# One core, a hybrid attention and mLSTM layer: three engines keep the source's order through the attention stretch

## The chip, the core and the metric

The kernel runs on one core of a Trainium2 chip. A core has a TensorE for matrix products (PE in the profile, its weight loads PEld), a VectorE (DVE), a ScalarE (ACT), a GpSimd (POOL) and a SyncE (SP), which issues the DMAs. Each of them works through its own list of instructions in the order in which they stand in it, and waits at an instruction until the semaphores that it names are there. The metric is the time of one execution on the device in microseconds (us); the figure for a kernel is the median of its runs.

## What is computed

A sequence of 2048 rows of 1024 numbers goes through one layer, in float32:

```python
h = rmsnorm(x, norm_g)
u = h @ w_in                                   # 1024 -> 7168, cut into q_a k_a v_a z_a x_m o_m z_m
# A: 8 heads of 128; three dilated causal windows, merged by their softmax denominators
att = sum(softmax(lses) * outs) * silu(z_a)
# B: 4 mLSTM heads of 256, chunk by chunk, with a state C handed on
num = inter * (q_t @ C) + p @ v_t
hm = sigmoid(o_m) * num / max(|den|, exp(-m_t))
hm = (hm - mean(hm)) * rsqrt(var(hm) + 1e-6) * hn_g
mls = hm * silu(z_m)
y = x + concat(att, mls) @ w_out
out = rmsnorm(y, final_g)
```

## The kernel before

The work has four stages. First the input projection with its normalisation, by seven products per block (the loop over `stream`); its results go to DRAM (`q_d`, `k_d`, `v_d`, `za_d`, `qm_d`, `xc_d`, `o_d`, `zm_d` and others). It ends at about 1241 us of the trace.

Second, attention beside the mLSTM, to about 1720 us. `attention` is a generator that runs through 256 units, 32 for each of 8 heads (16 blocks `b` for the local pattern, R = 0, and 16 for the dilated ones, R = 1, in turn). A unit `i` passes three steps: `qk` makes the scores (three products into a `pq` bank, L748 to L750), VectorE adds the bias and takes the row minimum (L752), ScalarE takes the exponential (L754); two units later `flip` transposes the result on TensorE (L762, into a `pt` bank) and ScalarE (L767) or VectorE (L765) copies it to `p`; one unit later `pv` multiplies it with the values (L780, into a `pm` bank). Of `pq`, `pt`, `pm` and `pu` there are two PSUM banks each. Once in eight units `qk_split` cuts the next quarter of q and k into a high and a low part: ScalarE makes the high ones (L620, L625), VectorE the low ones (L621, L626), GpSimd reorders q (L623). Per head, `head_stats` and `head_merge` combine the two patterns (L793 to L844).

`mlstm` is a second generator, stepped inside the first one's loop (L1243 and the lines behind it): 16 chunks of 128 rows, each in two `unit`s of nine pieces. A unit takes an exponential on ScalarE (`E`, L957, of what GpSimd cut out of `nb`, L944), products of q and k (L962, into `pt`), a transpose (L970) scaled by ScalarE into `kw` (L974), the outputs (L982, L985, into `pu`), which VectorE gates into `hm` (L986 to L990), and the new state `C` (L997 on TensorE, L1000 on VectorE). `norm`, run as `tail` beside the next chunk, normalises a chunk: small VectorE operations on `sm`, four squares on ScalarE (L1020), an inverse square root by three Newton steps of [128, 4] (L85 to L94), four multiplications of [128, 256] (L1031), and two sets of transposes (L1036, L1037).

Third, to about 2040 us, `early`: the mLSTM half of the output projection, block by block (L1142 to L1144, three products per piece), stepped beside the last attention units. It loads weights and mLSTM results into the two buffers `wor`, splits them on ScalarE and VectorE (L98, L99) into `we` and `me`, and from unit 230 on `load_wo` brings the weights of the other half, through the same two buffers. Fourth, the attention half and the last normalisation.

The generators fix only the order of the source. In what order the instructions of one engine are then listed is chosen by a list scheduler that knows the dependencies and its own estimate of each duration. The source also has a function `keep_order(start, engines)`, which chains all instructions of an engine behind `start` in source order; here it is called for the projection's start alone, with no engine in its list (`KO = ()`), so nothing is chained.

Of the kernel before, what the change touches and what calls it, by code (L numbers as in the profile page):

```python
# [8 lines left out]
F32 = mybir.dt.float32  # L9
# [18 lines left out]
def kernel(  # L28
# [52 lines left out]
    def rsqrt(pool, v, n):  # L81
# [5 lines left out]
        for c in (3.0, 12.0, 768.0):  # L87
            if n == 1:
                nc.vector.tensor_scalar(t, y, y, v, op0=ALU.mult, op1=ALU.mult)
            else:  # L90
                nc.vector.tensor_tensor(t, y, y, ALU.mult)
                nc.vector.tensor_tensor(t, t, v, ALU.mult)
            nc.vector.scalar_tensor_tensor(y, t, c, y, op0=ALU.subtract, op1=ALU.mult)
        nc.vector.tensor_scalar(y, y, -1.0 / 8192.0, None, op0=ALU.mult)  # L94
# [608 lines left out]
    def head_tiles(at, d):  # L703
# [3 lines left out]
        for n, shape, bufs in (("vn", [128, 16, 128], 2), ("vc", [128, 16, 128], 2), ("zs", [128, T], 1)):  # L707
            d[n] = at.tile(shape, F32, name=n, bufs=bufs)
# [7 lines left out]
        nc.sync.dma_start(d["zs"], za_d[h])  # L716
# [71 lines left out]
    def head_stats(at, d):  # L788
        h = d["h"]
        ps = pt.tile([128, 512], F32, name="pt")  # L790
# [61 lines left out]
    def attention(at):  # L852
# [9 lines left out]
        for i in range(len(units) + 3):  # L862
            if i < len(units):
                h, u = units[i]
                if i == 0:
# [4 lines left out]
                    qk_split(D_[0], 0)  # L870
                S_[i] = qk(at, D_[h], u)
            if 0 <= i - 2 < len(units):
                h, u = units[i - 2]
                s, n = S_[i - 2]
                P_[i - 2] = flip(at, D_[h], u, s, n)
# [40 lines left out]
    def mlstm(mp):  # L916
# [90 lines left out]
        def norm(c):  # L1007
# [14 lines left out]
            yield  # L1022
# [3 lines left out]
            rs = rsqrt(mp, sm[:, 3, :], 4)  # L1026
            nc.vector.tensor_tensor(sm[:, 3, :], rs, sm[:, 1, :], ALU.mult)
            yield
            for h in range(MH):
                hm = hms[h // 2][:, h % 2]  # L1030
                nc.vector.tensor_scalar(hm, hm, sm[:, 0, h:h + 1], sm[:, 3, h:h + 1], op0=ALU.add, op1=ALU.mult)  # L1031
            yield
            for p in range(2):
# [4 lines left out]
                yield  # L1038
# [6 lines left out]
        for c in range(NB):  # L1045
            SM[c] = mp.tile([128, 4, MH], F32, name="sm", bufs=2)
            for p in range(2):
                nxt = (c, 1) if p == 0 else (c + 1, 0)
                for n, _ in enumerate(unit(c, p, nxt if nxt[0] < NB else None)):
                    yield  # L1050
                    if tail and n % 2:
                        if next(tail, "end") == "end":
                            tail = None
                        else:
                            yield
# [6 lines left out]
    def raw_tile():  # L1062
# [3 lines left out]
        return woB.tile([128, 512], F32, name="wor", bufs=2)  # L1066
# [12 lines left out]
    def load_wo(e):  # L1079
        pool, tag, bufs = ((at, "vn", 2), (at, "vc", 2), (ax[0], "kh", 1), (pre, "k", 1),  # L1080
                           (at, "oL", 2), (at, "oR", 2), (at, "vn", 2), (at, "vc", 2))[e]
        t = pool.tile([128, 2, D], F32R, name=tag, bufs=bufs)
        for n in range(2):
            c = slice(n * 512, (n + 1) * 512)
            raw = raw_tile()
            nc.sync.dma_start(raw, w_out[e * 128:(e + 1) * 128, c])
            split(t[:, 0, c], t[:, 1, c], raw)
# [4 lines left out]
    def early():  # L1092
# [16 lines left out]
        def m_split(n, b, i):  # L1109
            t = M[n, b, i] = woB.tile([128, 2, 4, 128], F32R, name="me", bufs=3)  # L1110
# [8 lines left out]
        w_get(0, 0)  # L1119
        m_get(0, 0, 0)  # L1120
        w_split(0, 0)
        m_split(0, 0, 0)
        yield 0
        for e in range(1, 8):
            w_get(0, e)
            if e == 4:
                m_get(0, 0, 1)
                w_split(0, e)
                m_split(0, 0, 1)
            else:  # L1130
                w_split(0, e)
            if e % 2:
                yield 0
# [58 lines left out]
    def out_fin(pss, b):  # L1192
        xr = at.tile([128, 2, D], F32, name="zs")[:, 0] if b % 2 == 0 else at.tile([128, D], F32, name="wr")
# [22 lines left out]
    def out_last(pss, b):  # L1216
        xr = at.tile([128, 2, D], F32, name="zs")[:, 0] if b % 2 == 0 else at.tile([128, D], F32, name="wr")
        nc.sync.dma_start(xr, y_d[b * 128:(b + 1) * 128, :])
        s2 = at.tile([128, 2], F32, name="s2", bufs=2)
        for n in range(2):  # L1220
# [6 lines left out]
            if n == 0:  # L1227
# [9 lines left out]
    total, done, start, end, lag = 16 * 25, 0, 18, 180, 3  # L1237
# [5 lines left out]
                            ident[:8, 4:8, None].to_broadcast([8, 4, 128]), ALU.add)  # L1243
    work = attention(at)
# [22 lines left out]
    for _ in work:  # L1267
# [7 lines left out]
        i += 1  # L1275
    loads += [load_wo(e) for e in range(4, 8)]
# [86 lines left out]
```

## Time and profile before

| | |
|---|---|
| median of 3 runs | 2219.49 us (2218.13 to 2221.97) |
| the profiled execution | 2220.11 us, of which 2217.2 us are the span from first to last instruction |
| PE busy | 2126.7 us (96% of the span) |
| DVE busy | 1488.1 us (67%) |
| ACT busy | 942.8 us (43%) |
| POOL busy | 251.8 us (11%) |
| mean granted TensorE clock | 0.988 of 2.4 GHz |

A PE that is called busy need not be at its peak, since the ends of its records are modelled and a record that waits inside its span counts as busy. So the number of records in a stretch says more than the busy time, where the mixture is alike. The granted clock has two levels, 1.2 and 2.4 GHz; a mean of 0.87 over a stretch means that the lower one held for about a quarter of it.

### The profile page before, as it was taken

To read this page: it belongs to the slowest core of one execution; us is meant where nothing else is said; L and a number is where in the kernel's file an instruction comes from. 1 tells how busy PE (TensorE), PEld (TensorE's weight loads), DVE (VectorE), ACT (ScalarE), POOL (GpSimd) and SP (SyncE) were. 2 spreads that over 40 slices of the span, in tenths; PEclk is the share of its full clock that TensorE was granted. 3 is DMA by queue.
4 is the path that set the end of the run, shared out by engine and by line. 5 is a ranking of instruction groups with operands and counts; after the bars stand their busy time and mean duration, and the time that the engine had idled before them with its cause. 6 is when DMAs were issued, how large, how long until landed. Compare 5 with 4: busy or idle time off the path is not lost.

```text
span 2217.2 us, 32676 instructions
## 1 busy us (share of the span) xinstructions
PE 2126.7 (96%) x11826; PEld 1788.0 (81%) x11826; DVE 1488.1 (67%) x3050; ACT 942.8 (43%) x1905; POOL 251.8 (11%) x221
## 2 busy tenths in 40 slices
PE   5999999999999999999999999999898999999998
PEld 4777888998878888787779888888887788777886
DVE  8887768556696558576666578868777644643654
ACT  6433333333383223334344555655555645532221
POOL 2200000000000000000000223343342221210000
PEclk9999999999999999999999999999999999999999
DMA  4256343432263333343324677776675664565442
GB/s 154 95 177 190 114 159 115 158 114 101 90 204 133 114 114 105 125 138 115 133 77 160 186 203 208 213 234 188 195 211 178 192 184 157 173 193 176 162 138 86
DMA packets 278896, 341.52 MB, mean 154 GB/s; under 512 B 22224, under 2 KB 194704, under 8 KB 276688
## 3 DMA queue, kind: packets, MB, share of 16 engines
q1 hardware_dynamic: 277872, 338.85, 48.2%
q8 instruction: 93, 1.52, 0.3%
q10 hardware_dynamic: 864, 0.59, 0.1%
q14 instruction: 67, 0.55, 0.1%
HBM read 222.13 MB, written 117.24 MB: 153 GB/s over the span
## 4 chain that ended last, share of the span: by engine, by line
PE 74%; DVE 9%; DMA 8%; issue 5%; ACT 3%; POOL 1%; SPq 0%; ACTq 0%; DVEq 0%; POOLq 0%
PE pb L349 31%; PE pa L349 12%; PE pm L780 3%; PE pu L997 2%; PE pt L762 2%; PE pu L985 2%; DMA wor<-mls_d 2%; DMA wor<-in_w_out 1%; DMA k<-k_d 1%; PE aux L500 1%; PE aux L510 1%; PE pq L748 1%; PE pq L750 1%; PE pq L749 1%; PE pu L982 1%
## 5 line engine op out<-in xcount | busy, mean ns | idle before, releaser
L98 ACT ACTIVATE whi<-ws 128x1024 fp32r<-128x1024 f32 x140 | 148.2, 1059 | 376.5 <-PE pb L349 209.4
L99 DVE TENSOR_TENSOR wlo<-ws,whi 128x1024 fp32r<-128x1024 f32 x140 | 171.8, 1227 | 81.3 <-ACT whi L98 80.4
L139 DVE TENSOR_TENSOR ws<-w,w 128x1024 f32<-128x1024 f32 x140 | 172.1, 1229 | 24.0 <-DMA w<-in_w_in 22.4
L754 ACT ACTIVATE s<-s,st 128x256 f32<-128x256 f32 (+3 forms) x256 | 134.9, 527 | 76.0 <-DVE st L752 68.8
L411 DVE TENSOR_TENSOR o<-pb,o 128x1024 f32<-128x1024 f32 x84 | 102.8, 1224 | 92.9 <-PE pb L349 91.9
L752 DVE CUSTOM_DVE_ANT_0 s<-pq,bl 128x256 f32<-128x256 f32 (+3 forms) x256 | 114.2, 448 | 43.3 <-PE pq L750 32.0
L612 POOL COPY bl<-bl 128x256 f32<-128x256 f32 x8 | 6.4, 796 | 1150.5 <-DMA q<-q_d 1111.3
L767 ACT ACTIVATE p<-pt 128x256 f32<-128x256 f32 (+1 forms) x192 | 81.3, 424 | 105.7 <-PE pt L762 104.6
L762 PE MATMUL pt<-sc,s 128*128 128x128 f32 x568 | 107.7, 279 | 7.1 <-ACT p L767 5.3
L98 ACT ACTIVATE whi<-w 128x1024 fp32r<-128x1024 f32 x56 | 59.2, 1057 | 125.2 <-PE pb L349 118.7
L1142 PE MATMUL pu<-we,me 128*128 128x512 f32 x256 | 106.6, 417 | 5.3 <-ACT me L98 4.4
L411 DVE TENSOR_TENSOR o<-pa,o 128x1024 f32<-128x1024 f32 x56 | 68.4, 1221 | 62.8 <-PE pa L349 62.8
L1143 PE MATMUL pu<-we,me 128*128 128x512 f32 x256 | 102.1, 399 | 2.9 <-DVE me L99 2.9
L1144 PE MATMUL pu<-we,me 128*128 128x512 f32 x256 | 101.2, 395 | 0.0
L780 PE MATMUL pm<-p,vc 128*128 128x128 f32 x640 | 96.3, 281 | 3.3 <-DVE p L765 1.7
L404 ACT ACTIVATE o<-pb 128x1024 f32<-128x1024 f32 x84 | 84.9, 1016 | 15.6 <-DVE o L411 9.8
L780 PEld LDWEIGHTS pm<-p,vc 128*128 128x128 f32 x640 | 84.0, 195 | 7.0 <-ACT p L767 3.5
L99 DVE TENSOR_TENSOR wlo<-w,whi 128x1024 fp32r<-128x1024 f32 x56 | 68.3, 1220 | 27.5 <-ACT whi L98 27.5
L762 PEld LDWEIGHTS pt<-sc,s 128*128 128x128 f32 x568 | 72.7, 143 | 17.3 <-ACT p L767 6.7
L99 DVE TENSOR_TENSOR me<-wor,me 128x512 fp32r<-128x512 f32 x64 | 48.4, 758 | 56.0 <-ACT me L98 55.9
L780 PE MATMUL pm<-p,vn 128*128 128x128 f32 x496 | 78.7, 279 | 5.1 <-ACT p L767 5.1
L997 PE MATMUL pu<-v,kw 128*128 128x257 f32 x240 | 71.6, 401 | 9.4 <-DVE C L1000 4.8
(592 smaller groups left out, 6565.9 us busy)
## 6 DMA issues: line engine op xcount, KB each, us to landing
w<-in_w_in SPq DMA_DIRECT2D x112, 512.0 KB
wor<-mls_d SPq DMA_DIRECT2D x64, 256.0 KB
q_d<-o SPq DMA_DIRECT2D x8, 1024.0 KB
k_d<-o SPq DMA_DIRECT2D x16, 512.0 KB
vm_d<-vm SPq DMA_DIRECT2D x32, 256.0 KB
xc_d<-xc SPq DMA_DIRECT2D x32, 256.0 KB
qm_d<-qm SPq DMA_DIRECT2D x32, 256.0 KB
v_d<-o SPq DMA_DIRECT2D x8, 1024.0 KB
```

What stands on the lines that cost most here:

```text
L98: nc.scalar.activation(hi, raw, AF.Copy)
L99: nc.vector.tensor_tensor(lo, raw, f(hi), ALU.subtract)
L139: eng.tensor_tensor(s, a, b, ALU.add if sign > 0 else ALU.subtract)
L349: nc.tensor.matmul(out, lhsT, rhs, start=start, stop=stop, skip_group_check=True)
L411: nc.vector.tensor_tensor(dst, ps, src, op)
L752: nc.vector.tensor_tensor_reduce(s[:, :n], ps[:, :n], bias, 1.0, 3e38, ALU.add, ALU.min, accum_out=st[:, col:col + 1])
L754: nc.scalar.activation(s[:, :n], s[:, :n], AF.Exp, bias=st[:, col:col + 1], scale=-1.0, accum_out=st[:, 16 + col:17 + col])
L762: nc.tensor.transpose(pp[:, i * 128:(i + 1) * 128], s[:, i * 128:(i + 1) * 128], ident)
L780: nc.tensor.matmul(od, v, p[:, j * 128:(j + 1) * 128], start=j == 0, stop=j == m - 1)
L997: nc.tensor.matmul(u[:, 0:257], kw[:, 2 * i + e, :], v[:, i], start=True, stop=True)
L1142: nc.tensor.matmul(acc, m[:, 0, j], w[:, 0], start=e == 0, stop=False)
L1143: nc.tensor.matmul(acc, m[:, 1, j], w[:, 0], start=False, stop=False)
```

## The change

`keep_order` is called once more, behind the loop over the attention units, for TensorE, VectorE and ScalarE and all instructions since the first attention unit. GpSimd's and SyncE's lists are still the scheduler's. With it the source is written in another order:

- `flip` of unit i-2 stands ahead of `qk` of unit i.
- `norm` has 13 pieces where it had 7 (one Newton step or two multiplications in a piece), and each piece rides behind a piece of the next chunk's units, with no place of its own: a chunk now takes 18 places and not 25 (`total`).
- the gate tile `zs` is loaded in `head_stats`, when it is near its use.
- `load_wo` issues both its loads, lets two places pass, and then splits; it has two buffers of its own, `wol`. `me` has two buffers and not three.
- `early` asks for its first ten tiles two ahead of the split.

```diff
+    def rsqrt_steps(pool, v, n):
...
+        for c in (3.0, 12.0, 768.0):
+            nc.vector.tensor_tensor(t, y, y, ALU.mult)
+            nc.vector.tensor_tensor(t, t, v, ALU.mult)
+            nc.vector.scalar_tensor_tensor(y, t, c, y, op0=ALU.subtract, op1=ALU.mult)
+            yield
...
@@ head_tiles, head_stats
-        nc.sync.dma_start(d["zs"], za_d[h])
...
+        d["zs"] = at.tile([128, T], F32, name="zs")
+        nc.sync.dma_start(d["zs"], za_d[h])
@@ attention
+            if 0 <= i - 2 < len(units):
+                hf, uf = units[i - 2]
+                s, n = S_[i - 2]
+                P_[i - 2] = flip(at, D_[hf], uf, s, n)
+            if i < len(units):
                 S_[i] = qk(at, D_[h], u)
-            if 0 <= i - 2 < len(units):
-                h, u = units[i - 2]
-                s, n = S_[i - 2]
-                P_[i - 2] = flip(at, D_[h], u, s, n)
@@ norm
+            yield
             nc.vector.reciprocal(sm[:, 1, :], sm[:, 1, :])
...
-            yield
+                if h % 2:
+                    yield
...
-            rs = rsqrt(mp, sm[:, 3, :], 4)
+            yield
+            rs = yield from rsqrt_steps(mp, sm[:, 3, :], 4)
...
             for h in range(MH):
+                if h == 2:
+                    yield
@@ mlstm, the loop over the units
-                    if tail and n % 2:
-                        if next(tail, "end") == "end":
-                            tail = None
-                        else:
-                            yield
+                    if tail and next(tail, "end") == "end":
+                        tail = None
@@ raw_tile, load_wo
-        return woB.tile([128, 512], F32, name="wor", bufs=2)
+        return woB.tile([128, 512], F32, name="wol", bufs=2)
...
+        raw = [raw_tile() for _ in range(2)]
+        for n in range(2):
+            nc.sync.dma_start(raw[n], w_out[e * 128:(e + 1) * 128, n * 512:(n + 1) * 512])
+        yield
+        yield
@@ early
-            t = M[n, b, i] = woB.tile([128, 2, 4, 128], F32R, name="me", bufs=3)
+            t = M[n, b, i] = woB.tile([128, 2, 4, 128], F32R, name="me", bufs=2)
...
+        tiles = [("w", 0, e) for e in range(4)] + [("m", 0, 0, 0)] + [("w", 0, e) for e in range(4, 8)] + [("m", 0, 0, 1)]
+        for i in range(len(tiles) + 2):
+            if i >= 2:
+                (w_split if tiles[i - 2][0] == "w" else m_split)(*tiles[i - 2][1:])
+            if i < len(tiles):
+                (w_get if tiles[i][0] == "w" else m_get)(*tiles[i][1:])
+            if i % 2:
                 yield 0
@@ the main loops
-    total, done, start, end, lag = 16 * 25, 0, 18, 180, 3
+    total, done, start, end, lag = 16 * 18 + 14, 0, 18, 180, 3
...
+    begin2 = len(nc.cur_bb.bb.instructions)
     work = attention(at)
...
+    keep_order(begin2, (mybir.EngineType.PE, mybir.EngineType.DVE, mybir.EngineType.Activation))
```

Both kernels have the same instructions; only their order and some buffers differ. Three places follow. The lines of the changed kernel stand 12 to 21 below those of the kernel before.

VectorE in the second chunk's normalisation (L94 ends the inverse square root, L1031 is the four multiplications), before:

```order
L94 TENSOR_SCALAR rs_y_10953<-rs_y_10953 128x4
L989 SCALAR_TENSOR_TENSOR sm<-pu,gcol 128x1
L1000 SCALAR_TENSOR_TENSOR C<-C,decb,pu 128x257
L1027 TENSOR_TENSOR sm<-rs_y_10953,sm 128x4
L990 TENSOR_TENSOR sm<-sm,pu 128x1
L752 ISA s,st<-pq,bl 128x128
L752 ISA st 128x1
L765 COPY p<-pt 128x128
L1031 TENSOR_SCALAR hm<-hm,sm 128x256 x4
L1000 SCALAR_TENSOR_TENSOR C<-C,decb,pu 128x257 x2
L752 ISA s,st<-pq,bl 128x256
```

and now, where L108 is the old L94, L1052 the old L1031, L765 the old L752:

```order
L108 TENSOR_SCALAR rs_y_10997<-rs_y_10997 128x4
L1046 TENSOR_TENSOR sm<-rs_y_10997,sm 128x4
L1016 SCALAR_TENSOR_TENSOR C<-C,decb,pu 128x257
L1052 TENSOR_SCALAR hm<-hm,sm 128x256 x2
L778 COPY p<-pt 128x256
L765 ISA s,st<-pq,bl 128x256
L765 ISA st 128x1
L1052 TENSOR_SCALAR hm<-hm,sm 128x256 x2
L979 TENSOR_TENSOR E<-E,pt 128x256
L1058 TENSOR_TENSOR z<-z,pt 128x512
```

The four multiplications stood in one row, ahead of two state updates and of the next unit's minimum; now a unit's minimum stands between two and two.

ScalarE at the second `unit` of the third chunk (L957 is its `E`, L974 the `kw` of the unit ahead of it), at about 1316 to 1321 us of the trace before:

```order
L974 ACTIVATE kw<-pt,gcol 128x256 x2
L754 ACTIVATE s,st<-s,st 128x256
L957 ACTIVATE E<-E,gcol 128x128 x2
L767 ACTIVATE p<-pt 128x256
L620 ACTIVATE qh<-q 128x512
L625 ACTIVATE kh<-k 128x4x128
L754 ACTIVATE s,st<-s,st 128x128
```

and now (L973 the same `E`, L990 the `kw` of its own unit):

```order
L796 ACTIVATE oR<-pm 128x4x128
L973 ACTIVATE E<-E,gcol 128x128 x2
L767 ACTIVATE s,st<-s,st 128x256
L990 ACTIVATE kw<-pt,gcol 128x256 x2
L780 ACTIVATE p<-pt 128x256
L767 ACTIVATE s,st<-s,st 128x256 x2
L634 ACTIVATE qh<-q 128x512
L639 ACTIVATE kh<-k 128x4x128
```

`E` stood just behind the `kw` of the unit ahead of it; now it stands just ahead of the `kw` of its own unit, four attention units later (over all 64 the mean is about five).

TensorE in one attention unit of the second head, before:

```order
L748 MATMUL pq<-kh,qh 128x256
L749 MATMUL pq<-k,qh 128x256
L750 MATMUL pq<-kh,q 128x256
L762 MATMUL pt<-sc,s 128x128 x2
L780 MATMUL pm<-p,vc 128x128
L962 MATMUL pt<-q,xc 128x128 x4
```

and now:

```order
L775 MATMUL pt<-sc,s 128x128 x2
L761 MATMUL pq<-kh,qh 128x256
L762 MATMUL pq<-k,qh 128x256
L763 MATMUL pq<-kh,q 128x256
L793 MATMUL pm<-p,vc 128x128
L978 MATMUL pt<-q,xc 128x128 x4
```

The transposes of the older unit stand ahead of the new scores and not behind them.

## Rows read from the trace of the kernel before

**Rows 1.** Windows: start:end, length, PE, PEld, DVE, ACT, POOL busy (records), clock, DMA, GB/s.

```profile
1280.00:1320.00 40.00, 39.74 (x278) 36.58 (x276) 27.68 (x124) 27.16 (x83) 7.94 (x10) 1.00 0.74 212
1320.00:1360.00 40.00, 34.08 (x193) 29.58 (x193) 35.48 (x115) 18.56 (x58) 13.87 (x13) 0.87 0.60 180
1280.00:1700.00 420.00, 393.23 (x2568) 350.49 (x2567) 325.67 (x1244) 242.79 (x737) 140.29 (x134) 0.98 0.71 207
1700.00:1760.00 60.00, 53.78 (x317) 44.28 (x316) 42.85 (x113) 37.49 (x104) 21.21 (x17) 0.91 0.60 190
1880.00:1920.00 40.00, 36.70 (x221) 29.95 (x220) 28.69 (x70) 28.41 (x77) 12.51 (x8) 1.00 0.51 162
1920.00:2040.00 120.00, 112.70 (x498) 87.69 (x497) 52.85 (x90) 34.39 (x61) 15.96 (x10) 0.99 0.62 199
```

**Rows 2.** Waits of PE, 1240 to 1720: who waited for whom, us, times, longest.

```profile
PE pu L997 <- DVE C L1000: 4.8, 3, 2.9
PE pm L780 <- ACT p L767: 4.6, 3, 2.9
PE pu L997 <- DVE sm L990: 4.6, 4, 1.4
PE pt L762 <- ACT p L767: 3.6, 2, 2.2
PE pt L970 <- ACT p L767: 2.7, 1, 2.7
```

**Rows 3.** Timeline at 1319 to 1327: start, us, what, idle before and its releaser.

```profile
1319.48 0.69 ACT L957 ACTIVATE E<-E,gcol 128x128 f32<-128x128 f32 x2 [2.19 <-POOL E L944]
1320.99 0.69 DVE L621 SCALAR_TENSOR_TENSOR q<-q,qh 128x512 fp32r<-128x512 f32 x1 [2.21 <-ACT qh L620]
1321.02 1.60 POOL L623 CAST qr<-qh 128x512 fp32r<-128x512 f32 x1 [1.58 <-ACT qh L620]
1321.60 1.04 DVE L93 SCALAR_TENSOR_TENSOR rs_y<-rs_t,rs_y 128x4 f32<-128x4 f32 x1
1324.19 2.08 PE L997 MATMUL pu<-v,kw 128*128 128x257 f32 x4 [2.87 <-DVE C L1000]
1324.61 2.37 DVE L1031 TENSOR_SCALAR hm<-hm,sm 128x256 f32<-128x256 f32 x4
```

**Rows 4.** Waits of all engines, 1240 to 1720, columns as in rows 2.

```profile
POOL E L944 <- DMA nb<-nb_d: 63.5, 13, 13.0
ACT E L957 <- POOL E L944: 27.8, 20, 3.6
DVE k L626 <- ACT kh L625: 10.4, 6, 3.9
DVE q L621 <- ACT qh L620: 2.6, 3, 2.2
```

**Rows 5.** Line L93, 1240 to 1720: count, ns min/median/max, first and last start.

```profile
L93 DVE SCALAR_TENSOR_TENSOR rs_y<-rs_t,rs_y x48: 148/161/1368, 1287.6 to 1711.7; 128x4 f32<-128x4 f32 x48
```

**Rows 6.** Groups by line, VectorE, 1240 to 1720: count, busy, mean ns, idle before.

```profile
L621 DVE SCALAR_TENSOR_TENSOR q<-q,qh 128x512 fp32r<-128x512 f32 x22 | 16.2, 735 | 2.6 <-ACT qh L620 2.6
L93 DVE SCALAR_TENSOR_TENSOR rs_y<-rs_t,rs_y 128x4 f32<-128x4 f32 x48 | 11.9, 247 | 1.2
```

**Rows 7.** Timeline of ScalarE at the start of the attention, columns as in rows 3.

```profile
1241.74 1.67 ACT L625 ACTIVATE oR<-k 128x512 fp32r<-128x512 f32 x3 [3.38 <-PE pa L349]
1243.32 1.04 ACT L451 ACTIVATE o<-o 128x1024 f32<-128x1024 f32 x1
```

**Rows 8.** Timeline at 1900: a load into `wor`, and its split.

```profile
1900.47 0.37 SPq L1099 DMA_DIRECT2D wor<-in_w_out  x1
1903.83 0.63 ACT L98 ACTIVATE we<-wor 128x512 fp32r<-128x512 f32 x1 [2.06 <-DMA wor<-in_w_out]
```

**Rows 9.** Tile `wor`, 1240 to 2060: idle before its users until, us, times.

```profile
  DMA wor<-mls_d: 57.0, 24
  DMA wor<-in_w_out: 19.7, 14
```

More of the change, by code (lines that the diff above doesn't have):

```diff
@@ L93, in rsqrt @@
             nc.vector.scalar_tensor_tensor(y, t, c, y, op0=ALU.subtract, op1=ALU.mult)
+        nc.vector.tensor_scalar(y, y, -1.0 / 8192.0, None, op0=ALU.mult)
+        return y
+    def rsqrt_steps(pool, v, n):
+        y = pool.tile([128, n], F32, name=f"rs_y{n}", bufs=2)
+        t = pool.tile([128, n], F32, name=f"rs_t{n}", bufs=2)
+        yi = y.bitcast(mybir.dt.int32)
+        nc.vector.tensor_scalar(yi, v.bitcast(mybir.dt.int32), 1, None, op0=ALU.logical_shift_right)
+        nc.vector.tensor_scalar(yi, yi, -1.0, float(0x5F3759DF), op0=ALU.mult, op1=ALU.add)
+        for c in (3.0, 12.0, 768.0):
[3 more added lines that the diff above has]
+            yield
         nc.vector.tensor_scalar(y, y, -1.0 / 8192.0, None, op0=ALU.mult)
@@ L706, in head_tiles @@
         vd = v_d[h // 2]
-        for n, shape, bufs in (("vn", [128, 16, 128], 2), ("vc", [128, 16, 128], 2), ("zs", [128, T], 1)):
+        for n, shape, bufs in (("vn", [128, 16, 128], 2), ("vc", [128, 16, 128], 2)):
             d[n] = at.tile(shape, F32, name=n, bufs=bufs)
@@ L1050, in mlstm @@
                     yield
-                    if tail and n % 2:
-                        if next(tail, "end") == "end":
-                            tail = None
-                        else:
-                            yield
+                    if tail and next(tail, "end") == "end":
+                        tail = None
             for _ in tail or ():
@@ L1082, in load_wo @@
         t = pool.tile([128, 2, D], F32R, name=tag, bufs=bufs)
+        raw = [raw_tile() for _ in range(2)]
[3 more added lines that the diff above has]
+        yield
         for n in range(2):
             c = slice(n * 512, (n + 1) * 512)
-            raw = raw_tile()
-            nc.sync.dma_start(raw, w_out[e * 128:(e + 1) * 128, c])
-            split(t[:, 0, c], t[:, 1, c], raw)
+            split(t[:, 0, c], t[:, 1, c], raw[n])
             yield
@@ L1118, in early @@
         late = None
[L1119 to L1132, printed above, removed]
+        tiles = [("w", 0, e) for e in range(4)] + [("m", 0, 0, 0)] + [("w", 0, e) for e in range(4, 8)] + [("m", 0, 0, 1)]
[5 more added lines that the diff above has]
+            if i % 2:
                 yield 0
@@ L1192, in out_fin @@
     def out_fin(pss, b):
-        xr = at.tile([128, 2, D], F32, name="zs")[:, 0] if b % 2 == 0 else at.tile([128, D], F32, name="wr")
+        xr = at.tile([128, T], F32, name="zs")[:, 0:D] if b % 2 == 0 else at.tile([128, D], F32, name="wr")
         nc.sync.dma_start(xr, y_d[b * 128:(b + 1) * 128, :])
@@ L1216, in out_last @@
     def out_last(pss, b):
-        xr = at.tile([128, 2, D], F32, name="zs")[:, 0] if b % 2 == 0 else at.tile([128, D], F32, name="wr")
+        xr = at.tile([128, T], F32, name="zs")[:, 0:D] if b % 2 == 0 else at.tile([128, D], F32, name="wr")
         nc.sync.dma_start(xr, y_d[b * 128:(b + 1) * 128, :])
```

## The prediction

> **What bounds the kernel now.** I read the windows first, to see where TensorE loses time, then its waits, then one bad place in the timeline, then the waits of the other engines.
>
> The reader is to see in the windows that TensorE sets the pace. From 1280 to 1320 it is busy for 39.74 of 40 us at full clock and makes 278 records, so a record costs 40 / 278 = 0.144 us where nothing holds it up [rows 1]. From 1280 to 1700 there are 2568 records, which at that price are 370 us of the 420: 50 us are lost, though only 27 of them show as idle [rows 1]. The next 40 us after the good ones have 193 records (27.8 us) and a clock of 0.87 [rows 1]. There VectorE is busy for 35.48 of 40 us: it is the bound for a while, and over the whole stretch it is busy for 325.67 of 420, 78%, so it has room if its work comes evenly.
>
> Of the 50 us, TensorE's own waits name two groups: it waited for VectorE's `C` and `sm` 4.8 + 4.6 = 9.4 us, and for ScalarE's copies 4.6 + 3.6 + 2.7 = 10.9 us [rows 2] (these rows begin at 1240; the places lie behind 1280 but for small ones). The mean clock of 0.98 costs 2% of 420, 8.4 us [rows 1]. The other 21 us are small gaps and records that wait inside their span.
>
> The timeline shows how one such hole is made. ScalarE stood at `E` for 2.19 us, since GpSimd had not cut it out; behind it stood the split of q, for which VectorE waited 2.21 us; behind that stood the Newton steps and the four multiplications, 2.37 us in one row; and TensorE waited 2.87 us for the state [rows 3]. The first cause is a load: GpSimd waited 63.5 us for `nb`, ScalarE 27.8 us for GpSimd [rows 4].
>
> **The change part by part**, against the profiled execution's 2220.1 us (span 2217.2 and 2.9 around it), 0.6 above the median.
>
> 1. Thirteen pieces. The order shows two multiplications, a unit's minimum, two multiplications where there were four, two state updates and then the minimum. VectorE does as much as before; the wait of 2.87 us shrinks by about the half that it does not see at once. All of the 9.4 us could go, or one more wait of 2.9 could come where pieces meet a merge and a split. I take -7, nearer to the first end, since the other engines' work is unchanged; ends -9.4 and +2.9.
>
> 2. `E` in its source place. It stands some five units later in ScalarE's list, and SyncE, which is not chained, can issue the load as early as now. A unit lasts 420 us times 8 over the 160 units or so, about 2.6 us, so five of them cover 13 us, which is the longest wait of GpSimd for `nb` [rows 4]. The 27.8 us go, and with them the lateness of the copies: I take -9 of 10.9; ends -10.9 and 0. What is late next is the copy itself behind `kw` and the squares; it has the two units between scores and transposes as cover.
>
> 3. The clock falls after holes. If most of the holes go, I take -6 of the 8.4; ends -8.4 and 0. Of the 21 us of small gaps I take a third, -6, since in 1280 to 1320 there were none; ends -14 and 0.
>
> 4. The splits of q and k in their source places. Now the scheduler lets k's run long ahead and VectorE waits 10.4 + 2.6 = 13.0 us for them [rows 4]. In source order VectorE's low part stands right behind ScalarE's high one. A copy of that size took 0.63 us on ScalarE [rows 8]; 22 splits [rows 6] of at least one such wait are 14 us, of two (an exponential stands ahead) 28. So VectorE idles 1 to 15 us more; I take 8, and half of it on TensorE's path, as VectorE is the bound only in parts: +4; ends 0 and +15.
>
> 5. The start. In the new order ScalarE's four tanh of the output gate (1.04 each, 4.2 in all) stand between the first two units' exponentials, where three of the four ran ahead of the attention; three splits of k (1.67) leave that place [rows 7]. That is 2.5 us more, all on the path, as TensorE has nothing else there: +3; ends 0 and +5 (with the lower clock).
>
> 6. The change-over to `early`, 1700 to 1760. Its first ten tiles come in pairs through two buffers. A load took 3.4 us from issue to its split, the high part 0.63 [rows 8], the low one 0.74 (an operation of that size, [rows 6]): 4.8 us a pair, 24 us for five. ScalarE's list now has one attention unit between two pairs, so TensorE has some 11 records of 0.144, 1.6 us, in each 4.8, and stands for 16 us. Now it is idle for 6.2 there, and the clock of 0.91 takes 5.4 more [rows 1]; the last chunk's normalisation, which lay in one lump there, is spread now. So +4; ends -6 and +10.
>
> 7. `early` and `load_wo` with two buffers each. TensorE is idle 3.3 us from 1880 to 1920, where both go through the two `wor`, and 7.3 up to 2040 [rows 1]. I take half of it, -5; ends -10.6 and 0. The third `me` is not missed: its place is free once four of eight pieces are done, and a split takes 1.4 us. `zs` moves off SyncE's way by one load per head: nothing, as SyncE's list is ahead of its use in either.
>
> The transposes ahead of the scores: nothing. They need an exponential made two units earlier, and the copy starts one score (three records, 0.4 us) sooner; if ScalarE should run two units late, they would hold up the scores, which is the slower rival.
>
> The sum is -7 - 9 - 6 - 6 + 4 + 3 + 4 - 5 = -22: 2198.1 for the profiled execution, 2197.5 as a median. All good ends together would be -59, all bad ones +33; they do not come together. For the forecast's own range I go halfway from the sum to the good ones, 2180, and a third of the way to the bad ones, 2216; what lies beyond either belongs to the rivals.
>
> **The rivals.**
>
> *Most of the 50 us go.* If every stretch comes to what 1280 to 1320 shows, four fifths of 50 are won, with the -5 of `early` and the +11 of terms 4 to 6: 2186 or, with these at their good ends, 2165. For it: that stretch has the same mixture and needed no other work. Against it: VectorE's 78%, and only two banks of each kind between the engines.
>
> *Slower: ScalarE stands at a load with the exponentials behind it.* Place: the splits of `early`. Now ScalarE's users of `wor` wait 57.0 + 19.7 = 76.7 us in 38 places, 2.0 us each [rows 9], and TensorE loses only the idle 17 us of [rows 1] from 1700 to 2040, because the scheduler has put exponentials ahead. In source order each wait delays the exponentials behind it. What TensorE has in front of it are two units, 2 x 1.6 = 3.2 us: as long as the waits stay below that, nothing shows; above it each adds what goes beyond. If they double to 4.0, 38 x 0.8 = 30 us come, and with terms 1 to 3 kept at half (-14) and 4 and 5 (+7) the time is 2243; at half of the places 2228.
>
> *No change.* The scheduler's list may be as good as a list can be: two banks of each kind couple the engines to within a unit or two, and VectorE's heavy units stay heavy. Then the gains of 1 to 3 stay below 7 us and meet terms 4 to 6: 2220 within 4. For it: TensorE shows idle time in only 27 of 420 us [rows 1].
>
> *VectorE's small operations meet GpSimd.* One Newton operation on four columns took 1.04 us while GpSimd made a copy of 1.60 [rows 3]; the median of that line is 0.161, the longest 1.368 [rows 5], the mean 0.247 [rows 6], so its 48 lose 4 us, and with the two like it some 12 in all. GpSimd is busy for a third of the time [rows 1]. In one row, one meeting delays all; spread over 48 pieces with three operations or so, each meets one in three for half of 1.6 us, 13 us: the same. If each of the 144 were alone, it would be 38, 26 more, half of it on the path: +13, 2211. The Trainium skill (SBUF — State Buffer, section "SBUF: two separate sides") says that VectorE and GpSimd share a pair of ports under an exclusive lock, and that a VectorE operation with two SBUF inputs is shut out for the whole of a GpSimd one. By that rule, which speaks against spreading such operations, the mechanism is this rival's; the trace agrees in the 1.04 us.
>
> **How the numbers follow.** The forecast (2180 to 2216, all but its last us faster) has 0.50; most of the loss gone (2165 to 2186) 0.15; the GpSimd case 0.06; no change 0.13; slower 0.16. Two measurements can be told apart from about 0.2%, 4.4 us: faster is below 2215, slower above 2224. So faster 0.50 + 0.15 + 0.06 = 0.71, within 0.13, slower 0.16. The range leaves the slower case out and takes in the other cases, most of them: 2165 to 2226.
>
> **What would show it.** Right: no row of VectorE's four multiplications in one; ScalarE's wait for `E` below 5 us; TensorE's waits for `C`, `sm` and the copies together below 8; a clock of 0.99 or more from 1280 on; more than 2568 records in the same 420 us; TensorE idle for longer at the change-over. Wrong: VectorE's waits for ScalarE's high parts above 30 us with TensorE waiting behind them; ScalarE's waits for `wor` above 3 us each; a TensorE that waits at transposes for an exponential; holes that are as many as before but elsewhere.

## The result: the kept order is 6.3% slower

The changed kernel takes 2357.82 us (median of 4 runs, 2354.57 to 2365.89), the kernel before 2218.81 beside it. The ratio is 1.0629, with a 95% interval of 1.0600 to 1.0658. The forecast was 2197.5, and its slowest rival 2243.

The windows of the changed kernel (start:end, length, PE, PEld, DVE, ACT, POOL busy (records), clock, DMA, GB/s), to be read beside [rows 1]:

```profile
1280.00:1320.00 40.00, 35.54 (x237) 31.73 (x235) 24.91 (x86) 23.75 (x69) 11.89 (x11) 0.96 0.82 227
1440.00:1480.00 40.00, 30.72 (x162) 25.88 (x161) 27.14 (x99) 17.44 (x57) 9.96 (x9) 0.83 0.52 150
1280.00:1700.00 420.00, 351.50 (x2056) 301.62 (x2055) 285.80 (x990) 195.00 (x590) 124.45 (x108) 0.90 0.59 173
```

In the same 420 us TensorE makes 2056 records where it made 2568. At the 0.144 us of an unhindered record that is 296 us of work; 124 us are lost where 50 were. No engine has become the bound: VectorE falls from 325.67 to 285.80 us, ScalarE from 242.79 to 195.00. They all stand and wait. The clock falls from 0.98 to 0.90.

Where in the program the time goes is told by the 64 exponentials `E` of the mLSTM, one group of rows in each kernel (count, shortest, median and longest in ns, first and last start in us); the first row is the kernel before, the second the changed one:

```profile
L957 ACT ACTIVATE E<-E,gcol x64: 384/390/408, 1269.4 to 1681.7; 128x128 f32<-128x128 f32 x64
```

```profile
L973 ACT ACTIVATE E<-E,gcol x64: 384/386/403, 1274.1 to 1802.6; 128x128 f32<-128x128 f32 x64
```

The last of them starts 121 us later. So seven eighths of the 138 us by which the two traces differ in length arise beside the mLSTM. By the start of the scores, unit 176 is 120 us late and unit 192 is 134 us late; the rest changes little.

The waits of the changed kernel from 1240 to 1845 (who waited for whom: us, times, longest), to be read beside [rows 2, 4]:

```profile
PE pu L1013 <- DVE C L1016: 21.7, 14, 4.7
PE pt L986 <- DVE E L979: 12.5, 7, 4.8
PE pt L775 <- ACT s L767: 9.7, 6, 3.7
PE pu L1013 <- DVE sm L1006: 7.1, 5, 2.3
DVE hm L1002 <- PE pu L1001: 42.9, 42, 3.3
DVE s L765 <- PE pq L763: 34.3, 48, 2.5
DVE q L635 <- ACT qh L634: 30.1, 23, 2.6
ACT s L767 <- DVE st L765: 195.9, 135, 5.2
```

Of the last one the kernel before (1240 to 1720) has a quarter:

```profile
ACT s L754 <- DVE st L752: 47.0, 45, 4.3
```

TensorE waits for VectorE, VectorE for TensorE and ScalarE, ScalarE for VectorE. What one of the worst holes is made of, the timeline of the changed kernel shows (start, us, what, idle before and its releaser):

```profile
1444.59 0.40 ACT L767 ACTIVATE s<-s,st 128x128 f32<-128x128 f32 x1 [2.40 <-DVE st L765]
...
1444.99 0.61 ACT L634 ACTIVATE qh<-q 128x512 fp32r<-128x512 f32 x1
1445.51 0.61 ACT L639 ACTIVATE kh<-k 128x512 fp32r<-128x512 f32 x1
1445.64 0.69 DVE L635 SCALAR_TENSOR_TENSOR q<-q,qh 128x512 fp32r<-128x512 f32 x1 [1.08 <-ACT qh L634]
1445.67 1.61 POOL L637 CAST qr<-qh 128x512 fp32r<-128x512 f32 x1 [2.33 <-ACT qh L634]
1446.25 1.58 DVE L640 TENSOR_TENSOR k<-k,kh 128x512 fp32r<-128x512 f32 x1
1447.21 1.56 POOL L637 CAST qr<-q 128x512 fp32r<-128x512 f32 x1
1447.75 1.04 DVE L101 TENSOR_SCALAR rs_y<-sm 128x4 int32<-128x4 int32 x1
...
1449.51 0.47 DVE L1016 SCALAR_TENSOR_TENSOR C<-C,decb,pu 128x257 f32<-128x257 f32 x1
...
1450.04 0.80 PE L1013 MATMUL pu<-v,kw 128*128 128x257 f32 x1 [4.71 <-DVE C L1016]
```

This is a `qk_split`. In ScalarE's list it stands behind an exponential that waited 2.40 us for VectorE's minimum, and VectorE in turn stands 1.08 us until ScalarE has made q's high part. The same high part lets GpSimd start its reordering copy. So k's low part runs beside that copy and lasts 1.58 us, and the next operation, on four columns, runs beside the second copy and lasts 1.04. Behind them stand the Newton steps and then the state update, and TensorE stands 4.71 us for it. The lines of the low part of k, before and after:

```profile
L626 DVE TENSOR_TENSOR k<-k,kh x28: 677/690/1756, 1268.5 to 1760.7; 128x512 fp32r<-128x512 f32 x28
```

```profile
L640 DVE TENSOR_TENSOR k<-k,kh x28: 1570/1594/1758, 1303.3 to 2051.5; 128x512 fp32r<-128x512 f32 x28
```

It is not one bad meeting but all 28: the shortest is 1570 ns where the median was 690. Of the operations right behind them ten were stretched as well, by 0.85 us or more. The 16 that have an operand in PSUM were not: the state update took its usual 0.47 us beside the same copy. The scheduler had kept these operations apart, and the source sets them behind each other.

### The profile page after: what moved, and what is told of

It is laid out like the page before. It is cut to its first block, busy times and chain, and to the rows that moved or that the text cites. A ratio compares the mean times of both kernels' runs of the same rounds, so it can differ in the third digit from the quotient of the medians.

```text
span 2355.6 us, 32660 instructions
## 1 busy us (share of the span) xinstructions
PE 2181.9 (93%) x11826; PEld 1823.2 (77%) x11826; DVE 1533.6 (65%) x3050; ACT 944.3 (40%) x1905; POOL 272.9 (12%) x221
## 5 line engine op out<-in xcount | busy, mean ns | idle before, releaser
L765 DVE CUSTOM_DVE_ANT_0 s<-pq,bl 128x256 f32<-128x256 f32 (+3 forms) x256 | 114.8, 449 | 70.2 <-PE pq L763 60.3
L775 PE MATMUL pt<-sc,s 128*128 128x128 f32 x568 | 115.7, 297 | 46.1 <-ACT s L767 9.7
L775 PEld LDWEIGHTS pt<-sc,s 128*128 128x128 f32 x568 | 78.8, 151 | 76.7 <-issue 15.0
L1013 PE MATMUL pu<-v,kw 128*128 128x257 f32 x240 | 77.6, 428 | 36.0 <-DVE C L1016 21.7
L793 PEld LDWEIGHTS pm<-p,vc 128*128 128x128 f32 x640 | 90.2, 207 | 5.8 <-ACT p L780 3.4
L793 PE MATMUL pm<-p,vn 128*128 128x128 f32 x496 | 83.5, 294 | 1.8 <-ACT p L780 1.8
```

The lines of the kernel that those rows point to most:

```text
L765: nc.vector.tensor_tensor_reduce(s[:, :n], ps[:, :n], bias, 1.0, 3e38, ALU.add, ALU.min, accum_out=st[:, col:col + 1])
L775: nc.tensor.transpose(pp[:, i * 128:(i + 1) * 128], s[:, i * 128:(i + 1) * 128], ident)
L793: nc.tensor.matmul(od, v, p[:, j * 128:(j + 1) * 128], start=j == 0, stop=j == m - 1)
```

## The experiments

All are compared with the kernel before, run beside them on the same chip. There its median lay between 2221.78 and 2225.38 us, in the result above at 2218.81; so a difference of two medians in this table is good to some 5 us, and where two or three runs make a median, to some 10, as the intervals show.

| | median, us | ratio to before | 95% interval |
|---|---|---|---|
| a_free: changed source, no chain | 2233.96 | 1.0046 | 1.0028 to 1.0063 |
| a_act: ScalarE alone kept | 2246.61 | 1.0101 | 1.0054 to 1.0148 |
| a_pe: TensorE alone | 2257.87 | 1.0146 | 1.0099 to 1.0193 |
| a_dve: VectorE alone | 2270.18 | 1.0201 | 1.0153 to 1.0249 |
| a_pe_dve: TensorE and VectorE | 2279.44 | 1.0250 | 1.0191 to 1.0309 |
| a_dve_act: VectorE and ScalarE | 2317.23 | 1.0420 | 1.0354 to 1.0487 |
| a_chain_m: all three, to the mLSTM's end | 2341.46 | 1.0529 | 1.0470 to 1.0588 |
| b_chain_m: old source, chained as a_chain_m | 2349.12 | 1.0564 | 1.0486 to 1.0641 |
| x_late: all three, low parts a unit later | 2291.70 | 1.0312 | 1.0291 to 1.0333 |
| x_act: all three, copies on ScalarE | 2329.27 | 1.0471 | 1.0453 to 1.0490 |
| x_late_act: both | 2298.44 | 1.0336 | 1.0314 to 1.0358 |
| b_act: kernel before, copies on ScalarE | 2227.42 | 1.0013 | 0.9998 to 1.0028 |
| x_late_stats: x_late, merge's weights spread | 2303.45 | 1.0355 | 1.0319 to 1.0390 |
| x_late_7: x_late with seven pieces | 2312.88 | 1.0399 | 1.0366 to 1.0432 |
| b_13: kernel before with thirteen pieces | 2230.99 | 1.0024 | 1.0006 to 1.0043 |
| x_late_stats_m: x_late_stats, chains to the mLSTM's end | 2286.46 | 1.0275 | 1.0243 to 1.0308 |
| x_late_da: x_late, TensorE not kept | 2279.67 | 1.0266 | 1.0229 to 1.0303 |
| x_late_pa: x_late, VectorE not kept | 2277.55 | 1.0269 | 1.0231 to 1.0306 |

### Which chain costs

The engines in the one call are left out or changed; a_dve has this edit:

```diff
-    keep_order(begin2, (mybir.EngineType.PE, mybir.EngineType.DVE, mybir.EngineType.Activation))
+    keep_order(begin2, (mybir.EngineType.DVE,))
```

Expected of a_free, a_pe, a_dve and a_act, in this order:

> The changed source with the one call of keep_order behind the attention loop left out, so that the list scheduler orders all engines again. Theory 1 (the kept order costs the 138 us, the new source by itself little): 2205 to 2240 us. Theory 2 (the new source costs them: thirteen pieces that ride behind the units' pieces, a chunk in 18 places and not 25, transposes first): above 2300 us, as with the chain.

> The changed kernel, but only TensorE keeps the source's order; VectorE's and ScalarE's lists are the scheduler's. Theory 1a (VectorE's kept list is what makes TensorE wait, since most of TensorE's waits after the change name VectorE): TensorE's chain alone costs under 40 us, below 2260. Theory 1b (TensorE's own list is the bad one; it stands at products whose bank is not free while others could run): above 2300. Theory 1c (it takes two or three chained lists that wait for each other): 2220 to 2270, and so do the other two single ones.

> The changed kernel, but only VectorE keeps the source's order. Theory 1a (VectorE's list carries the loss: state updates, gates and the low parts of the split stand ahead of what TensorE waits for): above 2300 us, with TensorE's waits for C, E and sm of 40 us or more. Theory 1c (two or three chained lists that wait for each other): 2220 to 2270.

> The changed kernel, but only ScalarE keeps the source's order. A rival (ScalarE stands at each exponential until VectorE's minimum is there, 196 us after the change against 47 before, and holds up copies and kw behind it): above 2290 us. Theory 1a (VectorE's list carries it) and 1c (several lists): below 2260; ScalarE's wait is then only the echo of a late VectorE.

Without a chain the new source takes 2234, so some 124 us come with the chains (theory 1 holds); the source itself is 10 us slower than the kernel before beside it. Singly the chains of TensorE, VectorE and ScalarE cost 24, 36 and 13 us over that, 73 together, so some 50 more need two or three at once (theory 1c, with VectorE's chain at the edge of its range). ScalarE's own chain costs nothing that shows beside the mLSTM: in its trace unit 176 is 6.6 us behind the kernel before, in a_free's 9.9, although its waits for VectorE's minimum are twice those of before (97.7 us, 69.9 in a_free). Its cost comes at the change-over, where unit 192 is 26.1 us late, and 10.9 in a_free.

Expected of a_pe_dve and a_dve_act:

> The changed kernel with TensorE and VectorE kept in the source's order and ScalarE's list left to the scheduler. Singly the two cost 24 and 36 us over the same source without a chain (2234), so added up 2294. Theory 1c (the two lists lock into each other: VectorE waits at a gate for a product, TensorE at the next product for that gate, and neither may take other work): more than the sum, 2310 to 2345. Theory 1d (ScalarE is the missing third): 2285 to 2300.

> The changed kernel with VectorE and ScalarE kept in the source's order and TensorE's list left to the scheduler. Added up: 2234 + 36 + 13 = 2283 us. Theory 1c (it is TensorE and VectorE that lock): 2270 to 2290. Theory 1d (ScalarE's exponentials and VectorE's minima lock): above 2300.

I had the wrong pair. TensorE and VectorE give 2279, no more than their sum of 2294. VectorE and ScalarE give 2317, 34 us more than their sum (theory 1d, though I had looked for it at the exponentials). TensorE with ScalarE was not run on this source. What the second pair shares and the first does not is the split. The groups of VectorE's lines (count, busy us, mean ns, idle before), first with VectorE and TensorE kept, then with VectorE and ScalarE:

```profile
L635 DVE SCALAR_TENSOR_TENSOR q<-q,qh 128x512 fp32r<-128x512 f32 x25 | 18.0, 719 | 0.0
L640 DVE TENSOR_TENSOR k<-k,kh 128x512 fp32r<-128x512 f32 x22 | 15.7, 712 | 0.0
```

```profile
L635 DVE SCALAR_TENSOR_TENSOR q<-q,qh 128x512 fp32r<-128x512 f32 x25 | 19.4, 776 | 32.6 <-ACT qh L634 32.6
L640 DVE TENSOR_TENSOR k<-k,kh 128x512 fp32r<-128x512 f32 x21 | 33.5, 1594 | 0.0
```

With ScalarE free the scheduler makes the high parts some 20 us ahead: VectorE waits for none, and GpSimd's first copy is over when k's low part runs. With both kept, 32.6 us of waiting and 21 times 0.9 us of stretching come at once.

### Where, and whether the rearranged source is to blame

The call of a_chain_m stands in front of `woB`, where the mLSTM is over; b_chain_m has the same call in the source of before.

```diff
+    keep_order(begin2, (mybir.EngineType.PE, mybir.EngineType.DVE, mybir.EngineType.Activation))
     woB = ctx.enter_context(tc.tile_pool(name="woB", bufs=1))
...
-    keep_order(begin2, (mybir.EngineType.PE, mybir.EngineType.DVE, mybir.EngineType.Activation))
```

Expected of a_chain_m and b_chain_m:

> The changed kernel with the three chains ended where the mLSTM ends (in front of the loop that steps the output projection beside the last attention units), so that the last stretch is the scheduler's again. In the changed kernel's trace 120 of the 138 us are there when the mLSTM ends. By that: 2335 to 2345 us. If the chain in the last stretch only carries on what the first one began (unfinished work that is pushed into it): 2350 or more, no gain.

> The kernel before (seven pieces, 25 places in a chunk, transposes behind the scores) with the same three chains up to the end of the mLSTM. Theory A (what costs is any kept order of this loop; the pieces matter little): 2325 to 2360, as the changed source under the same chains. Theory B (thirteen pieces that ride behind the units' pieces overload VectorE's places): 2300 or less. Theory C (the rearrangement softens what the chain costs): above 2370.

As expected, the last stretch holds some 16 us of it. The old source under the same chains costs as much (theory A); the intervals overlap, so the rearrangement as a whole neither causes the loss nor cures it. The split has the same two signs in b_chain_m, a wait for q's high part and a long low part of k:

```profile
L626 DVE TENSOR_TENSOR k<-k,kh 128x512 fp32r<-128x512 f32 x24 | 34.4, 1442 | 0.0
L621 DVE SCALAR_TENSOR_TENSOR q<-q,qh 128x512 fp32r<-128x512 f32 x24 | 17.8, 741 | 32.0 <-ACT qh L620 32.0
```

In b_chain_m TensorE's longest group of waits is another one, for ScalarE's copies at `pv`:

```profile
PE pm L780 <- ACT p L767: 34.0, 20, 5.6
```

In the changed kernel that group is 1.8 us. The two sources also differ in where the flip stands, so moving it ahead is the likely reason, but it was not run alone.

### The split taken apart

x_late writes VectorE's low parts, and with them GpSimd's second copy, one unit later; x_act gives both reordering copies to ScalarE. The first lines are x_late's, the last x_act's.

```diff
+        kh_, kl_ = (residues(d[n])[:, :, g * 128:(g + 1) * 128] for n in ("kh", "k"))
+        nc.scalar.activation(kh_, f(kl_), AF.Copy)
+        nc.gpsimd.tensor_copy(residues(qr[:, 0, g % 2]), hi.rearrange("p (j r) -> p r j", r=4))
...
+        def low():
+            nc.vector.scalar_tensor_tensor(lo, f(lo), c, f(hi), op0=ALU.mult, op1=ALU.subtract)
+            nc.vector.tensor_tensor(kl_, f(kl_), f(kh_), ALU.subtract)
+            nc.gpsimd.tensor_copy(residues(qr[:, 1, g % 2]), lo.rearrange("p (j r) -> p r j", r=4))
+        return low
...
+                if low:
+                    low.pop()()
                 if R and b % 4 == slag:
...
+        nc.scalar.activation(residues(qr[:, 0, g % 2]), f(hi).rearrange("p (j r) -> p r j", r=4), AF.Copy)
...
+        nc.scalar.activation(residues(qr[:, 1, g % 2]), f(lo).rearrange("p (j r) -> p r j", r=4), AF.Copy)
```

Expected of x_late, x_act, x_late_act and b_act:

> The changed kernel, with the three chains, but VectorE's two low parts of a split (and GpSimd's copy of the low part of q) are written one attention unit later than ScalarE's two high parts. Theory 2a (the split is where the two lists lock: VectorE stands 1.3 us for ScalarE's high part, then its low part of k runs 1.59 us and not 0.69, since GpSimd's copy of the high part of q is at work at the same time; 2.2 us of VectorE for each of 28 splits, with TensorE's longest holes just behind): VectorE's wait for the high part below 3 us, the low part of k at 0.7 to 0.9 us, and 40 to 75 us off: 2282 to 2318. Theory 2b (VectorE has slack there, and the loss is made elsewhere by round trips between TensorE and VectorE): less than 20 us off, above 2338.

> The changed kernel, with the three chains, but the two reordering copies of a split are made by ScalarE and not by GpSimd, behind its two high parts; VectorE's low parts stay where they are and still wait for the high ones. It tells the two halves of theory 2a apart. If the meeting with GpSimd is most of it: the low part of k at 0.7 us, 20 to 45 us off (2312 to 2338), although ScalarE gets 1.2 us more in each split. If the wait is most of it: within 15 us of the changed kernel, and ScalarE's exponentials later.

> Both edits: low parts one attention unit later, and the copies on ScalarE. Theory 2a: at least as fast as the better of the two single edits, and near the kernel with TensorE and VectorE alone chained (2279): 2270 to 2300. What is left above the unchained source (2234) is then TensorE's and VectorE's own order. Theory 2b: above 2330.

> The kernel before, in the scheduler's order, with the two reordering copies of a split on ScalarE and not on GpSimd. In the trace of before VectorE's small operations stretch beside GpSimd's copies (1.04 us in place of 0.16). If that meeting costs TensorE time in the kernel before as well: 3 to 10 us off (2209 to 2216). If the scheduler's order has slack for it, or ScalarE's 34 us more weigh as much: 2216 to 2226.

Theory 2a holds. The low parts one unit later give 66 us back (2291.7). The groups of x_late and of x_act:

```profile
L640 DVE SCALAR_TENSOR_TENSOR q<-q,qh 128x512 fp32r<-128x512 f32 x25 | 23.7, 949 | 2.0 <-ACT qh L634 1.9
L641 DVE TENSOR_TENSOR k<-k,kh 128x512 fp32r<-128x512 f32 x22 | 20.0, 907 | 0.0
```

```profile
L638 DVE SCALAR_TENSOR_TENSOR q<-q,qh 128x512 fp32r<-128x512 f32 x24 | 18.5, 769 | 31.7 <-ACT qh L634 31.7
L639 DVE TENSOR_TENSOR k<-k,kh 128x512 fp32r<-128x512 f32 x21 | 14.3, 683 | 0.0
```

In x_late the wait has gone from 30.1 to 1.9 us and the mean of k's low part from 1597 to 907 ns. In x_act the wait stays at 31.7, the meeting alone is gone (683 ns), and 29 us come back, although ScalarE has two more copies in each split. That lies in the range that I had given for a meeting that is most of the loss; but x_late gives 66 and leaves a part of the meetings (q's low part has grown from 767 to 949 ns). So the meeting is worth some 29, net of ScalarE's extra work, and by difference the wait is the larger part; the wait was not taken away alone. Both edits together give no more than x_late (its interval and theirs overlap); ScalarE's extra copies are the likely reason, not shown by themselves. In the kernel before the same exchange makes no difference: there k's low part had a median of 690 ns as it was, so few of them met a copy.

### The pieces, a lump, and what is left

x_late_7 puts the old `norm`, its stepping and `16 * 25` into x_late; b_13 puts the new ones into the kernel before. x_late_stats spreads the twelve small operations that make a head's merge weights.

```diff
-            if i % 32 == 9 and i > 31:
+            if 9 <= i % 32 <= 12 and i > 31:
                 next(stats, None)
...
         nc.scalar.activation(w, w, AF.Exp)
+        yield
...
         nc.vector.reciprocal(m, m)
+        yield
...
+        yield
         wp = at.tile([64, 2, 2, 32], F32R, name="wp")
```

Expected of x_late_7 and b_13:

> The three chains with the low parts a unit later (2292 us), but a chunk is normalised in the seven pieces of the kernel before, with places of their own (25 a chunk). It prices the thirteen pieces where the order is kept and the split is out of the way. If shorter pieces help a kept order, as forecast (7 us and more): 2300 to 2325. If the pieces ride at the cost of the state updates beside them: 2280 or less. If neither: 2286 to 2298.

> The kernel before, in the scheduler's order, with only the normalisation changed: thirteen pieces that ride behind the units' pieces, 18 places a chunk. Without a chain the whole changed source costs about 10 us over the kernel before. If the pieces are the reason: 2226 to 2234. If they gain, as forecast for their part: 2208 to 2214. If they are nothing to a scheduler, which spreads the normalisation by itself: 2216 to 2224, and the 10 us belong to the other edits.

Thirteen pieces are worth 21 us where the order is kept: with seven, TensorE's wait for the gates' `sm` is 21.0 us in 13 places, while that for `C` falls from 20.0 to 6.3. In the scheduler's order they gain nothing: 0.24% slower, with an interval of 0.06 to 0.43%. That is about half of the 0.46% that the new source costs without a chain, and the intervals overlap; in the trace unit 176 is 9 us late, in a_free's 10.

Expected of x_late_stats and x_late_stats_m:

> The three chains with the low parts a unit later (2292 us), and in addition the weights of a head's merge (twelve small VectorE operations and an exponential between them, in one place of the source; 3.5 us of VectorE in a row, behind which a state update and then TensorE stood 3.9 us) are spread over four attention units. Theory 3a (what is left above the unchained source is lumps in VectorE's list; this one comes five times in the mLSTM's stretch and twice behind it): 10 to 20 us off, 2272 to 2282. Theory 3b (it is the fixed order of TensorE and VectorE as such): 2287 to 2295.

> All repairs together: low parts a unit later, the merge's weights spread, and the chains ended where the mLSTM ends. The last one gave 16 us in the changed kernel (2357.8 to 2341.5) and should give 8 to 16 here: 2262 to 2275 if the merge's part is worth 10 us or more, 2275 to 2285 if it is not. Below 2240 would say that a kept order can be as good as the scheduler's; above 2285 that the gains don't add up.

Theory 3a fell; the run lies above the range of 3b too, and not for the reason that 3b gives. The waits of TensorE, x_late first, then x_late_stats (both 1240 to 1780):

```profile
PE pu L1019 <- DVE C L1022: 20.0, 15, 3.9
```

```profile
PE pt L849 <- DMA wr<-wm_d: 18.2, 5, 5.9
PE pu L1022 <- DVE C L1025: 15.1, 16, 2.4
```

The lump did hold TensorE up: the wait for `C` falls by 5 us and its longest from 3.9 to 2.4. But the weights now leave three units later for DRAM and come back as `wr` too late for the product that spreads them, five times, once a head. In a kept list TensorE stands there for 18.2 us and may not take the scores that follow. Ending the chains early gives 17 us on top, and the whole stays at 2286: above 2285, where I had said the gains would not add up.

Expected of x_late_da and x_late_pa:

> The kernel with the low parts a unit later (2292 us with the three chains), with VectorE and ScalarE alone kept and TensorE's list left to the scheduler. What is left is 58 us above the unchained source (2234). Theory 4a (TensorE's fixed list carries most of it: it stands at a state product while scores or transposes could run): 2240 to 2258. Theory 4b (VectorE's fixed list carries most of it): 2275 to 2290. Theory 4c (they share it): 2258 to 2275.

> The same kernel with TensorE and ScalarE alone kept and VectorE's list left to the scheduler, which then may put state updates ahead of small operations. Theory 4a (TensorE's list): 2275 to 2290. Theory 4b (VectorE's list): 2240 to 2258. Theory 4c: 2258 to 2275; the chain of TensorE alone, on the changed source, cost 24 us and gave 2258.

Of the 58 us that x_late stays above 2234, releasing TensorE gives 12 and releasing VectorE 14, with intervals that overlap x_late's. With only one of the two kept, beside ScalarE, 44 to 46 us remain. Each run came out where I had put it if the list still kept was the bad one, so this pair does not tell which list is the worse one.

What the sums tell is this. With the split repaired the three chains cost 58 us, less than the 73 that they cost one by one without the repair, and the two pairs, 46 and 44, lie near their sums of 49 and 37. So the part that needed several lists at once has gone with the split, and what stays is of the size that each kept list costs by itself. From which operations that comes is not settled.

No version beats the kernel before.

## Why the prediction was wrong, point by point

**The failing step is 4, the split.** I took 1 to 15 us of idle VectorE and put half on the path, "as VectorE is the bound only in parts". The wait itself was nearly right: 30.1 us in 23 places, 1.3 each, just above my own count of 14 to 28. Its price was wrong, since three things were missing. GpSimd's copies start from the same high part, and stretch k's low part by 0.9 us each time and in ten of 28 splits the next operation by as much: 2.2 to 3.1 us a split in place of 0.6 to 1.3. Next, to put half on the path is wrong in a kept list, because the state update that TensorE needs stands behind the split and cannot pass it. And the 78% of VectorE's busy time that I read as room was room only for a list that may be reordered. Measured: 66 us for the repair, against +4 with an end of +15. My own sign for being wrong, waits for high parts above 30 us with TensorE behind them, is what came, by a hair; its price was not in the sum. The 58 us that x_late keeps over the unchained source had no term in the sum at all.

**GpSimd.** The rival on small VectorE operations named the right mechanism and the wrong partner: I looked at Newton steps beside copies as the scheduler had placed them [rows 3], and not at which operations the source places beside a copy. In the hole above GpSimd's first copy started with q's low part and lasted 1.61 us, 0.5 longer than the 1.10 of a free one; k's low part then ended 0.55 us behind it. The Trainium skill (SBUF — State Buffer, section "SBUF: two separate sides") says that VectorE, in a 2-port mode or with two SBUF inputs, and GpSimd, where it reads SBUF, need the same pair of ports, and that the one that starts first has it for the whole instruction. The trace agrees: 0.69 us of work took 1.58.

**Step 1, the pieces.** Forecast -7. I misread the hole that it starts from. In [rows 3] TensorE's wait of 2.87 us ends at 1324.19, when the state update is done, and the four multiplications start only at 1324.61:

```profile
1322.91 0.78 DVE L94 TENSOR_SCALAR rs_y<-rs_y 128x4 f32<-128x4 f32 x1
...
1323.67 0.47 DVE L1000 SCALAR_TENSOR_TENSOR C<-C,decb,pu 128x257 f32<-128x257 f32 x1
```

What stood ahead of the update were a wait for q's high part and two small operations that ran beside GpSimd's copies, 1.04 and 0.78 us: the same hole as in the changed kernel, once. Where the order is kept, the thirteen pieces are worth 21 us (x_late_7), more than forecast; against the scheduler's list, which is what the sum was made against, they gain nothing (b_13). The row of four multiplications is gone, as expected, but TensorE's waits for `C` and `sm` rose from 9.4 to some 29 us in the changed kernel.

**Step 2, `E`.** ScalarE's 27.8 us for GpSimd are gone to the last one. The 9 us did not come: TensorE's waits for ScalarE's copies are 13.3 us in the changed kernel (four groups, the longest 7.5), 11.7 before (10.9 and two small groups). The "times 8" in this step is a slip: 420 us over 160 units are the 2.6. What I named as next was the copy behind `kw`; what came was the exponential behind a late minimum, 195.9 us.

**Step 3, clock and small gaps.** The sign turned with the holes: 10% of 420 us at the lower clock's price, 42, in place of 8.4. Slower TensorE records behind the holes are part of the losses above.

**Step 5, the start.** +3 forecast; unit 16 is 7 us late, 5 more than in a_free. **Step 6, the change-over.** +4 forecast, with an end of +10; 14 us by the scores of units 176 to 192, and 16 by a_chain_m. The step had the right place and was too small. **Step 7, `early`.** -5 forecast; from unit 192 to the end the changed kernel takes 480 us, the one before 475: no gain, and a_free takes 480 as well, so the chains are not the reason.

**The slower rival** had the sign and not the place. The waits of users of `wor` in the changed kernel (1840 to 2180):

```profile
  DMA wor<-mls_d: 23.2, 10
  DMA wor<-in_w_out: 8.8, 8
```

They are 32.0 us in 18 places, down from 76.7 in 38 [rows 9]; the weights that moved to `wol` add 0.8. Which of the edits to the loads did it was not run. Waiting at the head of a fixed list came at VectorE, far earlier.

**The range** ended at 2226 and left the slower rival out; but all bad ends together, +33, and that rival's 2243 stay over 100 us short as well, since they bound seven small edits. (The lower end, 2165, is 2163 by its own terms; nothing hangs on it.) The edit that mattered had no term: that three lists may not be reordered at all. [rows 3] showed one chain of waits across four engines, and I read it as a fault of the scheduler's order, where both source orders, once kept, make it at split after split.

## What to carry to other kernels

Price a kept order as a change of its own, engine by engine and in pairs: here 24, 36 and 13 us singly were 124 together. In such a list look for the places where one engine's result is used by the next one in the next line of the source, put a unit of other work between them, and look at what a third engine starts from the same result. A busy share of 78% was no reserve for an engine whose list was fixed, and short pieces helped only there.

## What the runs showed of the hardware

A VectorE subtraction of 128x512 in SBUF took 683 to 690 ns alone and 1594 beside a GpSimd copy that was already running; the copy itself took 1.10 us alone and 1.61 when a VectorE operation of that kind ran at its start. A VectorE operation with an input in PSUM ran beside the copy at its usual time (the state update, 0.47 us). The profile counts the whole of it as busy, so VectorE's busy time grew from 1488.1 to 1533.6 us with no more work: the 28 low parts show 0.9 us each, 25 in all, that no wait row names. TensorE's mean granted clock over 1280 to 1700 was 0.98 before, 0.90 with three kept lists, 0.96 with the split repaired: the lower of its two levels followed holes in its work. In the hole shown above it set in, and held from 1448.8 to 1455.5. Over a stretch it does not go in step with the loss: a_pe_dve has 0.93 with 2256 records, a_dve_act 0.96 with 2197.
